# A decoder layer on one core: the eighth pair of the up projection in seven products, with its weight sums formed during the attention and kept in DRAM

## The chip, the core and the metric

The kernel runs on one core of a Trainium2 chip. The core has five engines that run their own instruction streams and meet at semaphores: TensorE (PE: matmuls, with the weight loads in front of them), VectorE (DVE), ScalarE (ACT), GpSimd (POOL) and SyncE (SP), which in this kernel issues nearly all DMAs. Each stream is worked off in the order in which it was built. The metric is the device time of one execution in microseconds (us); lower is better.

## The reference

```python
def reference(x, norm_attn_g, w_in, ..., w_up, w_down):
    h = rmsnorm(x, norm_attn_g)
    proj = einsum('bsd,de->bse', h, w_in)      # q_a k_a v_a | q_b k_b v_b
    o_a = swa_attention(q_a, k_a, v_a, sinks, rel_bias)
    o_b = stick_breaking_attention(q_b, k_b, v_b)
    x = x + concat(rmsnorm(o_a), rmsnorm(o_b)) @ w_out
    h = rmsnorm(x, norm_mlp_g)
    return x + square(relu(h @ w_up)) @ w_down
```

All is float32, with 512 tokens, D = 2048, an MLP width of 8192, and 16 heads of 64 in each of the two groups.

## The kernel before

Each float32 operand of a large product is split into a rounded part `hi` (a copy on ScalarE) and a rest `lo` (a subtraction on VectorE, line 92, or 106 in the first projection). A product is then three matmuls: hi·hi, hi·lo, lo·hi.

**Attention.** `w_in` is read in chunks of two 128-row blocks by 512 columns, `st` (pool `wst`, four buffers), which `wchunk` loads on the SP queue and splits. The stages in order: `kv`, `qa0`, `qa1`, `v0`, two of `qk`, `v1`, two of `qk`; eight chunks each, with 24 matmuls of 512 columns to a chunk. The four results of a stage stand in the four PSUM banks of pool `pp`; the next stage's matmuls write the same banks once VectorE has evacuated them (`f_q`, line 319, for `qa0`). The scores and softmaxes of earlier stages are woven in by `pump`. Before the first softmax the relative-position bias is written to DRAM as a skewed table (`skew`, 3 MB, one DMA on the ACT queue) and read back on the SP queue (`bias`, line 425). The scheduler of the framework, not the program text, settles where each instruction stands in its engine's stream.

**Up projection.** The 16 blocks of 128 rows of `w_up` go in eight pairs (k = 0 to 7), the 8192 columns in 32 groups g of 256. Half of the tokens (256) times two blocks of rows and two of columns is a 2x2 by 2x2 block product. For k = 0 to 6 it is done in seven block products in place of eight (`U_PRODUCTS`), with sums of weight blocks formed by GpSimd (`u_sums`, line 779, four operations) and sums of activation blocks formed once (`turn_x2`, line 754). For k = 7 (`PLAIN`) it is done in eight (`U_PLAIN`). So a group has 7 x 21 + 24 = 171 matmuls of 256 columns. `u_load` fetches two pairs in one DMA (`st_u`, tag `st`, four buffers), `u_sums` forms the sums of two pairs in `s_u` (two buffers; for k = 7 none, so half the width for that tile), `u_split` splits. `u_finish` puts the banks of the group before together, squares the positive part, forms sums for the next product and stores hi and lo to DRAM (`ac`).

**Down projection.** Seven products again, with weight sums by GpSimd (`T1` to `T4`, line 931); the first of them are formed while the last group of the up projection still runs.

Of the kernel before, what the change touches and what calls it, by code (L numbers as in the profile page):

```python
# [12 lines left out]
F32 = mybir.dt.float32  # L13
# [7 lines left out]
P = 128  # L21
# [37 lines left out]
def hymba_layer(ctx: ExitStack, tc: tile.TileContext, x, norm_attn_g, w_in, q_norm_g, k_norm_g,  # L59
# [304 lines left out]
    const.tile([P, 32], F32, name="pad_left")  # L364
# [332 lines left out]

    HP = T // 2
    KP = KD // 2
    PLAIN = KP - 1  # L700
# [15 lines left out]
    def evac_b(n, t, ps):  # L716
# [4 lines left out]
        xs = xw.tile([P, 512], F32, tag="xs", bufs=8, name=f"xs2_{n}{t}")  # L721
# [15 lines left out]
    def turn_x2(n, kk, banks):  # L737
# [3 lines left out]
        for r in range(2):  # L741
# [5 lines left out]
            nc.scalar.mul(out=hq[:, 1:3] if r else hq[:, 0:4:3] if k == PLAIN else hq[:, 0::7],  # L747
                          in_=tr.rearrange("p (b t) -> p b t", b=2), mul=g)
        nb = 4 if k == PLAIN else 7
        hi = hp[k].tile([P, nb, HP], F32R, name=f"h2h{k}")  # L750
        lo = hp[k].tile([P, nb, HP], F32R, name=f"h2l{k}")
        if k != PLAIN:
            for o, a, b in ((3, 7, 0), (4, 2, 3), (5, 2, 7), (6, 1, 4)):
                nc.vector.tensor_tensor(out=hq[:, o], in0=hq[:, a], in1=hq[:, b], op=ALU.subtract)
        split(hq[:, 0:nb], hi, lo)
# [4 lines left out]
    raws, sums, parts_u = {}, {}, {}  # L760
# [8 lines left out]
    def u_sums(i):  # L769
        if i < G * KP // 2:  # L770
            w = raws[i]
            s_ = sp.tile([P, 2, 4, P], F32, tag="s", name=f"s_u{i}")
            if i % (KP // 2) == PLAIN // 2:
                w, s_ = w[:, 0:1], s_[:, 0:1]
            for o, a, b, op in ((s_[:, :, 0], w[:, :, 0], w[:, :, 2], ALU.add),
                                (s_[:, :, 2], w[:, :, 1], w[:, :, 0], ALU.subtract),
                                (s_[:, :, 1], s_[:, :, 0], w[:, :, 1], ALU.subtract),
                                (s_[:, :, 3], w[:, :, 3], s_[:, :, 1], ALU.subtract)):
                nc.gpsimd.tensor_tensor(out=o, in0=a, in1=b, op=op)  # L779
# [16 lines left out]

    U_PLAIN = ((1, 0, 1, 0), (3, 1, 1, 0), (1, 3, 3, 0), (3, 2, 3, 0), (0, 0, 3, 1), (2, 1, 3, 1), (0, 3, 0, 1),
               (2, 2, 0, 1))
    U_PRODUCTS = ((0, 0, 0, 0), (2, 1, 1, 0), (1, 6, 3, 1), (3, 3, 2, 0), (5, 5, 2, 1), (4, 4, 1, 1), (6, 2, 3, 0))

    def u_products(i, ps):
# [3 lines left out]
        for a, b, n, half in U_PLAIN if k == PLAIN else U_PRODUCTS:  # L805
# [9 lines left out]
    def u_finish(g, ps, ew):  # L815
# [3 lines left out]
        p1 = ew.tile([P, HP], F32, tag="p1", name=f"p1_{g}")  # L819
        e = ew.tile([P, 5, HP], F32, tag="e", name=f"e{g}")  # L820
        u = ew.tile([P, 2, HP], F32, tag="u", name=f"u{g}")
        nc.scalar.copy(out=p1, in_=w[:, 0])
        nc.vector.tensor_tensor(out=e[:, 1::3], in0=p1.rearrange("p (o t) -> p o t", o=1).broadcast_to([P, 2, HP]),
                                in1=x_, op=ALU.add)
# [168 lines left out]
    for g in range(1, G):  # L993
        finishing = u_finish(g - 1, ps, ew)
        ps = u_banks(g)
        for k in range(KP):
            if g == G - 1:
# [3 lines left out]
                elif k == 4:  # L1001
                    d_sum(0, "T1")
# [86 lines left out]
```

## Time and profile before

| | |
|---|---|
| median of 3 runs | 2043.79 us (2041.43 to 2044.12) |
| profiled execution, its own time | 2043.11 us |
| its span, first to last instruction | 2041.0 us |
| TensorE busy | 2004.0 us, 98% of the span |
| VectorE, ScalarE, GpSimd busy | 1626.8, 1014.5, 1020.3 us |
| mean granted TensorE clock | 0.996 |

The profiled execution lies 0.7 us under the median. A busy time is the union of an engine's instructions; matmuls overlap, so the time from one matmul's start to the next is what a matmul costs, not its own duration. Times in the rows count from the start of the span.

### The profile page before, as it was taken

The numbers are of one execution on the slowest core, as the hardware profiler recorded it, in microseconds if no ns is written. First come the engines' busy times: TensorE is split into PE (matmuls) and PEld (weight loads), VectorE is DVE, ScalarE is ACT, GpSimd is POOL, SyncE is SP. The second block draws the span as 40 slices with busy tenths as digits, with TensorE's granted clock in tenths as the row PEclk, the third lists the DMA queues.
The fourth block names the chain that finished last, engine by engine and source line by source line (L and its number), as shares of the span: only waits on it lengthen the run. The fifth ranks groups of instructions, "written<-read, shape, count | busy, mean of one in ns | idle before, by whom it ended". The sixth has DMA issues, their size and how long they took to land. (4 is left out here: it accounts for less than half of the span.)

```text
span 2041.0 us, 31132 instructions
## 1 busy us (share of the span) xinstructions
PE 2004.0 (98%) x11748; PEld 1725.3 (85%) x11748; DVE 1626.8 (80%) x2034; ACT 1014.5 (50%) x1676; POOL 1020.3 (50%) x904
## 2 busy tenths in 40 slices
PE   8999999999999999999999999998999999999998
PEld 7887787778677889999999999997788888888887
DVE  4378646665775578999999999998989999999987
ACT  6267534544553565555555555554543333333343
POOL 0014332222320127777777777775756556655654
PEclk9999999999999999999999999999999999999999
DMA  6742332223345555665656565656756557456351
GB/s 220 123 129 85 100 93 81 73 92 111 107 134 186 168 166 182 203 203 183 203 182 205 182 205 182 206 182 264 273 223 227 177 216 267 155 226 258 145 186 62
DMA packets 213914, 350.30 MB, mean 172 GB/s; under 512 B 9779, under 2 KB 154372, under 8 KB 206596
## 3 DMA queue, kind: packets, MB, share of 16 engines
q1 hardware_dynamic: 211216, 345.02, 49.8%
q10 hardware_dynamic: 2548, 3.30, 1.3%
q8 instruction: 92, 1.51, 0.3%
q14 instruction: 58, 0.48, 0.1%
HBM read 270.16 MB, written 78.12 MB: 171 GB/s over the span
## 5 line engine op out<-in xcount | busy, mean ns | idle before, releaser
L811 PE MATMUL ps_u<-h2h,lo_u 128*128 128x256 f32 x1824 | 515.9, 283 | 6.3 <-DVE lo_u L92 6.3
L810 PE MATMUL ps_u<-h2l,hi_u 128*128 128x256 f32 x1824 | 514.7, 282 | 2.4 <-DVE h2l L92 2.4
L809 PE MATMUL ps_u<-h2h,hi_u 128*128 128x256 f32 x1824 | 514.8, 282 | 0.1
L1053 PE MATMUL ps_d<-hi_d,ad 128*128 128x512 f32 x896 | 353.4, 394 | 3.4 <-ACT U L969 1.6
L1054 PE MATMUL ps_d<-lo_d,ad 128*128 128x512 f32 x896 | 353.4, 394 | 1.2 <-DVE lo_d L92 1.2
L1055 PE MATMUL ps_d<-hi_d,ad 128*128 128x512 f32 x896 | 353.2, 394 | 0.0
L811 PEld LDWEIGHTS ps_u<-h2h,lo_u 128*128 128x128 f32 x1824 | 346.7, 190 | 7.5 <-DVE lo_u L92 6.7
L810 PEld LDWEIGHTS ps_u<-h2l,hi_u 128*128 128x128 f32 x1824 | 346.6, 190 | 2.9 <-DVE h2l L92 2.8
L809 PEld LDWEIGHTS ps_u<-h2h,hi_u 128*128 128x128 f32 x1824 | 346.6, 190 | 0.3 <-ACT h2h L91 0.3
L779 POOL TENSOR_TENSOR s_u<-st_u 128x256 f32<-128x256 f32 (+1 forms) x256 | 200.1, 801 | 252.3 <-DVE lo_u L92 181.2
L92 DVE TENSOR_TENSOR lo_d<-T,hi_d 128x1024 fp32r<-128x1024 f32 x128 | 241.4, 1899 | 38.1 <-ACT hi_d L91 37.4
L931 POOL TENSOR_TENSOR T<-st_d,T 128x1024 f32<-128x1024 f32 x64 | 169.1, 2645 | 201.0 <-DVE lo_d L92 198.5
L91 ACT CAST hi_d<-T 128x1024 fp32r<-128x1024 f32 x128 | 134.4, 1051 | 203.0 <-PE ps_d L1055 177.6
L92 DVE TENSOR_TENSOR lo_u<-st_u,hi_u 128x384 fp32r<-128x384 f32 (+1 forms) x256 | 218.2, 853 | 4.4 <-ACT hi_u L91 4.3
L1053 PEld LDWEIGHTS ps_d<-hi_d,ad 128*128 128x128 f32 x896 | 167.9, 187 | 44.6 <-ACT U L969 2.1
L92 DVE TENSOR_TENSOR lo_d<-st_d,hi_d 128x1024 fp32r<-128x1024 f32 x96 | 193.5, 2028 | 13.7 <-ACT hi_d L91 13.2
L1054 PEld LDWEIGHTS ps_d<-lo_d,ad 128*128 128x128 f32 x896 | 168.0, 188 | 42.0 <-DVE lo_d L92 2.0
L1055 PEld LDWEIGHTS ps_d<-hi_d,ad 128*128 128x128 f32 x896 | 168.0, 187 | 40.1
L92 DVE TENSOR_TENSOR lo_u<-s_u,hi_u 128x512 fp32r<-128x512 f32 x224 | 178.1, 795 | 1.0 <-ACT hi_u L91 1.0
L91 ACT CAST hi_u<-s_u 128x512 fp32r<-128x512 f32 x224 | 138.5, 618 | 78.7 <-POOL s_u L779 78.6
L91 ACT CAST hi_d<-st_d 128x1024 fp32r<-128x1024 f32 x96 | 100.6, 1050 | 152.2 <-PE ps_d L1055 140.6
L779 POOL TENSOR_TENSOR s_u<-st_u,s_u 128x256 f32<-128x256 f32 (+1 forms) x128 | 167.8, 1311 | 10.0
(223 smaller groups left out, 3825.7 us busy)
## 6 DMA issues: line engine op xcount, KB each, us to landing
st_u<-in_w_up SPq DMA_DIRECT2D x128, 512.0 KB, 4.5
st_d<-in_w_down SPq DMA_DIRECT2D x64, 1024.0 KB, 8.3
ad<-ac SPq DMA_DIRECT2D x56, 1024.0 KB, 5.1
ac<-ah SPq DMA_DIRECT2D x32, 896.0 KB, 6.3
ac<-al SPq DMA_DIRECT2D x32, 896.0 KB, 6.6
st_qk<-in_w_in SPq DMA_DIRECT2D x64, 256.0 KB, 3.0
st_o<-in_w_out SPq DMA_DIRECT2D x32, 512.0 KB, 4.5
st_qa<-in_w_in SPq DMA_DIRECT2D x16, 512.0 KB, 4.1
```

The lines of the kernel that those rows point to most:

```text
L91: nc.scalar.copy(out=hi, in_=st)
L92: nc.vector.tensor_tensor(out=lo, in0=st, in1=hi.bitcast(F32), op=ALU.subtract)
L779: nc.gpsimd.tensor_tensor(out=o, in0=a, in1=b, op=op)
L809: nc.tensor.matmul(o, wh[:, a], hh[:, b], start=first, stop=False, skip_group_check=True)
L810: nc.tensor.matmul(o, wh[:, a], hl[:, b], start=False, stop=False, skip_group_check=True)
L811: nc.tensor.matmul(o, wl[:, a], hh[:, b], start=False, stop=(k == KP - 1), skip_group_check=True)
L931: nc.gpsimd.tensor_tensor(out=o, in0=raw[cj, a, h], in1=raw[cj, b, h], op=ALU.subtract)
L1053: nc.tensor.matmul(o, al, bh[:, kk], start=first, stop=False, skip_group_check=True)
L1054: nc.tensor.matmul(o, al, bl[:, kk], start=False, stop=False, skip_group_check=True)
L1055: nc.tensor.matmul(o, ar, bh[:, kk], start=False, stop=end, skip_group_check=True)
```

## The change

The eighth pair is done in seven products too. Its weight sums (one tile of 128 x 4 x 128 for each of the 32 column groups) are formed by GpSimd from an extra load of the two row blocks of `w_up`, stored to a DRAM table `us`, and loaded in the up projection into the half of `s_u` that stood empty. The program text calls `sum_ahead` at every second chunk of the eight stages after `kv`, once per column group. `turn_x2` forms the activation sums of the eighth pair as for the others. `u_finish` works in one tile `a` in place of `p1`, `e`, `u` and `a`, with one addition less. `T1` of the first down tile is ordered behind the last weight sums. Some pads and one buffer count (`xs`, 8 to 5) make room.

```diff
+    us = dram.tile([DFF // 256, P, 4, P], F32, name="us")
+    ahead_g = iter(range(DFF // 256))
+    pre = attn.enter_context(tc.tile_pool(name="pre", bufs=2, side="right"))
+
+    def sum_ahead():
+        g = next(ahead_g, None)
+        if g is None:
+            return
+        r = pre.tile([P, 4, P], F32, tag="r", name=f"pr{g}")
+        nc.sync.dma_start(out=r.rearrange("p (k r) c -> p k (r c)", k=2),
+                          in_=w_up.rearrange("(k p) c -> p k c", p=P)[:, KD - 2:KD, g * 256:(g + 1) * 256])
+        z = pre.tile([P, 4, P], F32, tag="z", name=f"ps_{g}")
+        block_sums(r, z)
+        nc.sync.dma_start(out=us[g], in_=z)
+
+    def block_sums(w, z):
+        for o, a, b, op in ((0, w[..., 0, :], w[..., 2, :], ALU.add), (2, w[..., 1, :], w[..., 0, :], ALU.subtract),
+                            (1, z[..., 0, :], w[..., 1, :], ALU.subtract),
+                            (3, w[..., 3, :], z[..., 1, :], ALU.subtract)):
+            ins = nc.gpsimd.tensor_tensor(out=z[..., o, :], in0=a, in1=b, op=op)
+        return ins
...
             hi, lo = wchunk(src(c), f"{name}{c}", perm)
+            if c % 2:
+                sum_ahead()
...
-            if i % (KP // 2) == PLAIN // 2:
-                w, s_ = w[:, 0:1], s_[:, 0:1]
...
+            if i % (KP // 2) == KP // 2 - 1:
+                nc.sync.dma_start(out=s_[:, 1], in_=us[i // (KP // 2)])
+                last_sum[0] = block_sums(w[:, 0], s_[:, 0])
+            else:
+                last_sum[0] = block_sums(w, s_)
...
-            if i % KP == PLAIN:
-                split(w, hi[:, 0:4], lo[:, 0:4])
-                return
...
-        for a, b, n, half in U_PLAIN if k == PLAIN else U_PRODUCTS:
+        for a, b, n, half in U_PRODUCTS:
...
-        nc.vector.tensor_tensor(out=e[:, 3], in0=e[:, 3], in1=w[:, 1], op=ALU.add)
...
-                    d_sum(0, "T1")
+                    with tc.issue_after(last_sum[0].ins):
+                        d_sum(0, "T1")
```

**Where the scheduler puts it.** First the SP queue, from the last chunks of `qa0` on; before, it reads (st_qa0_7 is the last chunk of `qa0`, st_qa1_0 the first of `qa1`):

```order
L111 DMA st_qa0_6_853<-in_w_in 128x2x512
L111 DMA st_qa0_7_885<-in_w_in 128x2x512
L425 DMA bias0_1193<-skew_580 128x256 x2
L425 DMA bias1_1363<-skew_580 128x256 x2
L111 DMA st_qa1_0_957<-in_w_in 128x2x512
```

Now the loads (pr0 to pr31, from `w_up`) and stores (tile names ps_0 to ps_31, to `us`) of all 32 sets begin behind the second chunk of `qa0`, take turns with its other chunks up to set 11, and end ahead of `bias`:

```order
L111 DMA st_qa0_1_669<-in_w_in 128x2x512
L307 DMA pr0_677<-in_w_up 128x2x256
L111 DMA st_qa0_2_737<-in_w_in 128x2x512
L307 DMA pr1_777<-in_w_up 128x2x256
L311 DMA us_582<-ps_0_679 128x512
L307 DMA pr2_849<-in_w_up 128x2x256
L111 DMA st_qa0_3_769<-in_w_in 128x2x512
L311 DMA us_582<-ps_1_779 128x512
```

```order
L307 DMA pr30_4927<-in_w_up 128x2x256
L311 DMA us_582<-ps_29_4849 128x512
L307 DMA pr31_5083<-in_w_up 128x2x256
L311 DMA us_582<-ps_30_4929 128x512
L311 DMA us_582<-ps_31_5085 128x512
L452 DMA bias0_1253<-skew_580 128x256 x2
L452 DMA bias1_1431<-skew_580 128x256 x2
L111 DMA st_qa1_0_993<-in_w_in 128x2x512
```

Nothing is spread over the later stages: 64 DMAs stand between the second chunk of `qa0` and the first of `qa1`. On GpSimd all 128 additions likewise stand ahead of its first work for the attention (hl_k0). The streams of PE, VectorE and ScalarE are the same as before up to the up projection. On VectorE the evacuations of `qa0` (f_q00, f_q01) stand behind the splits of the first three chunks of `qa1`, before and now:

```order
L106 TENSOR_TENSOR lo_qa0_7_916<-st_qa0_7_913,hi_qa0_7_915 128x512 x2
L106 TENSOR_TENSOR lo_qa1_0_996<-st_qa1_0_993,hi_qa1_0_995 128x512 x2
L106 TENSOR_TENSOR lo_qa1_1_1028<-st_qa1_1_1025,hi_qa1_1_1027 128x512 x2
L106 TENSOR_TENSOR lo_qa1_2_1124<-st_qa1_2_1121,hi_qa1_2_1123 128x512 x2
L346 SCALAR_TENSOR_TENSOR f_q00_953<-ps_qa0_0_617,rbc_514 128x512
L346 SCALAR_TENSOR_TENSOR f_q01_962<-ps_qa0_1_618,rbc_514 128x512
```

So these too come behind the 64 DMAs, through the loads of st_qa1_0 to st_qa1_2. The third place is VectorE in the first group of the up projection, between the splits of the seventh and the eighth activation pair (h2l6, h2l7). Before:

```order
L92 TENSOR_TENSOR h2l6_7121<-hq6_7107,h2h6_7120 128x1792
L92 TENSOR_TENSOR lo_u7_7207<-st_u3_6919,hi_u7_7206 128x512
L92 TENSOR_TENSOR lo_u8_7239<-st_u4_7012,hi_u8_7238 128x384
L92 TENSOR_TENSOR lo_u8_7239<-s_u4_7174,hi_u8_7238 128x512
L92 TENSOR_TENSOR h2l7_7169<-hq7_7155,h2h7_7168 128x1024
```

Now:

```order
L92 TENSOR_TENSOR h2l6_7383<-hq6_7369,h2h6_7382 128x1792
L92 TENSOR_TENSOR lo_u7_7473<-st_u3_7180,hi_u7_7472 128x384
L92 TENSOR_TENSOR lo_u7_7473<-s_u3_7336,hi_u7_7472 128x512
L92 TENSOR_TENSOR lo_u8_7507<-st_u4_7273,hi_u8_7506 128x384
L779 TENSOR_TENSOR hq7_7417<-hq7_7417 128x256 x3
L92 TENSOR_TENSOR lo_u8_7507<-s_u4_7440,hi_u8_7506 128x512
L779 TENSOR_TENSOR hq7_7417<-hq7_7417 128x256
L92 TENSOR_TENSOR lo_u9_7534<-st_u4_7273,hi_u9_7533 128x384
L92 TENSOR_TENSOR lo_u9_7534<-s_u4_7440,hi_u9_7533 128x512
L92 TENSOR_TENSOR h2l7_7431<-hq7_7417,h2h7_7430 128x1792
```

Four additions, one more weight split and the split of lo_u9 have come ahead of h2l7, and h2l7 is wider. At the end of the up projection GpSimd's T1_00 and T1_01, which stood ahead of the sums s_u126 and s_u127, now stand behind s_u127.

## Rows read from the trace of the kernel before

**Rows 1.** The page's head: span, and busy time of each engine.

```profile
span 2041.0 us, 31132 instructions
PE 2004.0 (98%) x11748; PEld 1725.3 (85%) x11748; DVE 1626.8 (80%) x2034; ACT 1014.5 (50%) x1676; POOL 1020.3 (50%) x904
```

**Rows 2.** SP queue in order of time, 20 to 116 us: start, length, issue.

```profile
27.04 31.05 SPq L111 DMA_DIRECT2D st_qa<-in_w_in  x7
64.57 0.37 SPq L111 DMA_DIRECT2D st_qa<-in_w_in  x1
95.52 1.76 SPq L425 DMA_DIRECT2D bias<-skew  x4
97.39 15.12 SPq L111 DMA_DIRECT2D st_qa<-in_w_in  x8
```

**Rows 3.** The SP queue's own waits, 60 to 100 us: total, times, longest.

```profile
SPq L425 <- DMA skew<-rv: 30.6, 1, 30.6
```

**Rows 4.** Timeline of ACT, DVE and PE, 84 to 108 us, with idle time ahead.

```profile
86.06 1.14 ACT L105 CAST hi_qa<-st_qa 128x512 fp32r<-128x512 f32 x2 [4.58 <-DMA st_qa<-in_w_in]
101.72 1.14 ACT L105 CAST hi_qa<-st_qa 128x512 fp32r<-128x512 f32 x2 [14.51 <-DMA st_qa<-in_w_in]
...
106.28 1.28 DVE L319 SCALAR_TENSOR_TENSOR f_q<-ps_qa,rbc 128x512 f32<-128x512 f32 x2
...
107.57 0.39 PE L116 MATMUL ps_qa<-hT,hi_qa 128*128 128x512 f32 x1
```

**Rows 5.** GpSimd's timeline, 745 to 749 us: one set of sums on 128x128.

```profile
746.14 0.88 POOL L779 TENSOR_TENSOR s_u<-st_u 128x128 f32<-128x128 f32 x2 [12.44 <-DVE lo_u L92]
746.99 0.46 POOL L779 TENSOR_TENSOR s_u<-s_u,st_u 128x128 f32<-128x128 f32 x1
747.52 0.74 POOL L779 TENSOR_TENSOR s_u<-st_u,s_u 128x128 f32<-128x128 f32 x1
```

**Rows 6.** DMA issues by line: count, size, us from issue to landing.

```profile
st_qk<-in_w_in SPq DMA_DIRECT2D x64, 256.0 KB, 3.0
oscr<-o SPq DMA_DIRECT2D x14, 256.0 KB, 2.0
```

**Rows 7.** Stretches: busy time of each engine, granted clock, DMA share, GB/s.

```profile
core 0: us, PE busy (x) PEld busy (x) DVE busy (x) ACT busy (x) POOL busy (x), PEclk, DMA share, GB/s
64.00:80.00 16.00, 16.00 (x76) 13.30 (x75) 8.09 (x15) 7.89 (x14) 1.16 (x1) 1.00 0.88 102
80.00:86.00 6.00, 6.00 (x28) 4.99 (x27) 2.49 (x3) 1.14 (x2) 2.89 (x2) 1.00 0.99 185
740.00:1390.00 650.00, 646.61 (x5424) 644.78 (x5423) 587.36 (x791) 368.57 (x612) 477.90 (x502) 1.00 0.60 194
1397.70:1404.50 6.80, 5.77 (x27) 5.77 (x28) 5.57 (x6) 4.35 (x4) 2.95 (x2) 0.50 0.25 87
```

**Rows 8.** GpSimd's timeline in the up projection: the same tile in following groups.

```profile
851.22 0.89 POOL L779 TENSOR_TENSOR s_u<-st_u 128x128 f32<-128x128 f32 x2
...
892.12 0.88 POOL L779 TENSOR_TENSOR s_u<-st_u 128x128 f32<-128x128 f32 x2
```

**Rows 9.** Instructions by line and shape: count | busy us, mean ns | idle before.

```profile
L92 DVE TENSOR_TENSOR lo_u<-st_u,hi_u 128x384 fp32r<-128x384 f32 x224 | 180.1, 804 | 4.4 <-ACT hi_u L91 4.3
L92 DVE TENSOR_TENSOR lo_u<-s_u,hi_u 128x512 fp32r<-128x512 f32 x224 | 178.1, 795 | 1.0 <-ACT hi_u L91 1.0
L92 DVE TENSOR_TENSOR lo_u<-st_u,hi_u 128x512 fp32r<-128x512 f32 x32 | 38.1, 1191 | 0.0
L754 DVE TENSOR_TENSOR hq<-hq 128x256 f32<-128x256 f32 x28 | 15.6, 596 | 0.4
```

**Rows 10.** VectorE's timeline, 756 to 769 us: splits of the last two activation pairs.

```profile
757.09 2.19 DVE L92 TENSOR_TENSOR h2l<-hq,h2h 128x1792 fp32r<-128x1792 f32 x1 [1.81 <-ACT h2h L91]
...
762.07 1.22 DVE L92 TENSOR_TENSOR h2l<-hq,h2h 128x1024 fp32r<-128x1024 f32 x1 [0.25 <-ACT h2h L91]
```

**Rows 11.** Waits, 1380 to 1410 us: total, times, longest.

```profile
PE ps_u L811 <- DVE lo_u L92: 6.3, 2, 5.4
```

More of the change, by code (lines that the diff above doesn't have):

```diff
@@ L363, in hymba_layer @@
     oscr = dram.tile([2 * 8, P, T], F32, name="oscr")
-    const.tile([P, 32], F32, name="pad_left")
+    const.tile([P, 24], F32, name="pad_left")
     sm.tile([P, 32], F32, tag="pad", bufs=1, name="pad_small")
@@ L523, in v_group @@
             hi, lo = wchunk(src(c), f"v{o}_{c}")
+            if c % 2:
+                sum_ahead()
             for t in range(NT):
@@ L699, in hymba_layer @@
     KP = KD // 2
-    PLAIN = KP - 1
     G = DFF // 256
@@ L720, in evac_b @@
         nc.sync.dma_start(out=x2scr[n, :, t], in_=xt)
-        xs = xw.tile([P, 512], F32, tag="xs", bufs=8, name=f"xs2_{n}{t}")
+        xs = xw.tile([P, 512], F32, tag="xs", bufs=5, name=f"xs2_{n}{t}")
         nc.scalar.activation(out=xs, in_=xt, func=AF.Square, accum_out=ss2[:, t, n:n + 1])
@@ L746, in turn_x2 @@
             g = gT[:, 16 + 2 * k + r:17 + 2 * k + r]
-            nc.scalar.mul(out=hq[:, 1:3] if r else hq[:, 0:4:3] if k == PLAIN else hq[:, 0::7],
+            nc.scalar.mul(out=hq[:, 1:3] if r else hq[:, 0::7],
                           in_=tr.rearrange("p (b t) -> p b t", b=2), mul=g)
[L749 to L755, printed above, removed]
+        hi = hp[k].tile([P, 7, HP], F32R, name=f"h2h{k}")
+        lo = hp[k].tile([P, 7, HP], F32R, name=f"h2l{k}")
+        for o, a, b in ((3, 7, 0), (4, 2, 3), (5, 2, 7), (6, 1, 4)):
+            nc.vector.tensor_tensor(out=hq[:, o], in0=hq[:, a], in1=hq[:, b], op=ALU.subtract)
+        split(hq[:, 0:7], hi, lo)
         h2[k] = hi, lo
     wu = w_up.rearrange("(k p) c -> p k c", p=P)
-    raws, sums, parts_u = {}, {}, {}
+    raws, sums, parts_u, last_sum = {}, {}, {}, [None]
     def u_load(i):
@@ L772, in u_sums @@
             s_ = sp.tile([P, 2, 4, P], F32, tag="s", name=f"s_u{i}")
-            if i % (KP // 2) == PLAIN // 2:
-                w, s_ = w[:, 0:1], s_[:, 0:1]
[L775 to L779, printed above, removed]
+            if i % (KP // 2) == KP // 2 - 1:
[3 more added lines that the diff above has]
+                last_sum[0] = block_sums(w, s_)
             sums[i] = s_
@@ L793, in u_split @@
             split(s_, hi[:, 3:7], lo[:, 3:7])
-    U_PLAIN = ((1, 0, 1, 0), (3, 1, 1, 0), (1, 3, 3, 0), (3, 2, 3, 0), (0, 0, 3, 1), (2, 1, 3, 1), (0, 3, 0, 1),
-               (2, 2, 0, 1))
     U_PRODUCTS = ((0, 0, 0, 0), (2, 1, 1, 0), (1, 6, 3, 1), (3, 3, 2, 0), (5, 5, 2, 1), (4, 4, 1, 1), (6, 2, 3, 0))
@@ L818, in u_finish @@
         w, x_, y, z = [b.rearrange("p (h t) -> p h t", h=2) for b in ps]
[L819 to L824, printed above, removed]
+        a = ew.tile([P, 8, HP], F32, tag="a", name=f"a{g}")
+        nc.scalar.copy(out=a[:, 7], in_=w[:, 0])
+        nc.vector.tensor_tensor(out=a[:, 1:5:3], in0=a[:, 7:8].broadcast_to([P, 2, HP]), in1=x_, op=ALU.add)
         yield
-        nc.vector.tensor_tensor(out=u, in0=e[:, 4:5].broadcast_to([P, 2, HP]), in1=y, op=ALU.add)
+        nc.vector.tensor_tensor(out=a[:, 5:7], in0=a[:, 4:5].broadcast_to([P, 2, HP]), in1=y, op=ALU.add)
         yield
-        nc.vector.tensor_tensor(out=e[:, 0:4:2], in0=u, in1=z, op=ALU.add)
-        nc.vector.tensor_tensor(out=e[:, 3], in0=u[:, 1], in1=y[:, 0], op=ALU.add)
-        nc.vector.tensor_tensor(out=e[:, 3], in0=e[:, 3], in1=w[:, 1], op=ALU.add)
-        a = ew.tile([P, 8, HP], F32, tag="a", name=f"a{g}")
-        nc.scalar.activation(out=a[:, 0:4], in_=e[:, 0:4], func=AF.Relu)
+        nc.vector.tensor_tensor(out=a[:, 0:4:2], in0=a[:, 5:7], in1=z, op=ALU.add)
+        nc.vector.tensor_tensor(out=a[:, 3], in0=a[:, 6], in1=y[:, 0], op=ALU.add)
+        nc.scalar.activation(out=a[:, 0:4], in_=a[:, 0:4], func=AF.Relu)
         yield
```

## The prediction, made before the changed kernel had run

> **What bounds the kernel now.** I read the head of the profile first [rows 1]: TensorE is busy for 2004.0 of the 2041.0 us of the span, so it sets the pace nearly everywhere, and time can be won only by giving it fewer matmuls, or lost by making it wait. The profiled execution took 2043.11 us, 2.1 more than its span and 0.7 under the median; the sum below starts from 2043.1. Then I looked at the two places that the change touches. In the middle of the up projection (the stretch from 740 to 1390) [rows 7] TensorE is busy for 646.6 of 650 us at granted clock 1.00, and VectorE for 587.4 (90%), GpSimd for 477.9. One tile of sums comes back on GpSimd after 40.90 us [rows 8], which is two column groups, so a group takes 20.45 us. It has 171 matmuls: 119.6 ns each. In the attention, the order of instructions in the section on the change puts 64 new DMAs on the SP queue between the second chunk of `qa0` and `bias`. So I read that queue's stretch and the end of `qa0` closely [rows 2 to 4]: this is where a stall could arise.
>
> **What is removed: 11.5 us.** Each of the 32 groups loses one block product of three matmuls: 32 x 3 x 119.6 ns = 11.5 us. This holds only if TensorE stays the pace. VectorE now works 587.4/650 x 20.45 = 18.5 us a group. For the eighth pair it splits 128x384 and 128x512 (0.80 + 0.80 us) in place of one 128x512 of 1.19 [rows 9], +0.4 us, and saves a small addition that I don't count. 18.9 us against TensorE's new 20.09 is 94%: VectorE stays under it, and I take the whole 11.5. With VectorE as the pace instead it would be between 0 and 11.5.
>
> **What is added in the attention: a stall of TensorE.** First, what is queued behind the new DMAs. SP works its list off in order: the first `bias` DMA waited 30.6 us for `skew` [rows 3], went out at 95.52, and the loads of the chunks of `qa1`, behind it, only from 97.39 [rows 2], though their buffers were free long before. The first of these chunks reached ScalarE at 101.72 (14.51 us idle, waiting for that DMA), VectorE splits three chunks and then evacuates `qa0` at 106.28, 0.64 us for each of the two, and TensorE, which needs the freed bank, goes on at 107.57 [rows 4]. The first evacuation ended at 106.92, so there are 0.6 us to spare. If `bias` goes out at B in place of 95.52, TensorE waits B - 96.1.
>
> Second, the price of a set of sums. GpSimd's four additions on 128x128 took 2.12 us from 746.14 to 748.26 [rows 5]. The load has the 256 KB of a chunk, 3.0 us from issue to landing [rows 6]. There are two buffers, and in SP's list the load of set g+1 stands behind the store of set g-1, so it is not issued before the sums of g-1 are done. Two chains thus take turns, each with store issue 0.47 (four `bias` DMAs in 97.39 - 95.52), landing 3.0 and sums 2.12: 5.6 us for two sets, 2.8 for one. The additions alone (0.88 + 0.46 + 0.74, less a little overlap) make 1.84 to 2.1, the floor; my estimate of a high price is 3.35 (sums of 2.5 while VectorE works too, landing of 3.7 under load).
>
> Third, when they run. The first load follows the first chunks (from 27.04 on), at about 28.6 by my estimate; loads of `w_in` lie in front of it, so that its sums end about 36. Taking turns with the chunks of `qa0`, about nine sets should be through by 66. Now `skew` moves on another queue from about 64 to 95.2. The last chunk of `qa0`, issued at 64.57 [rows 2], reached ScalarE only at 86.06, which had waited for it [rows 4]: 21 us in place of 3. The DMA engines were taken at 0.88 and moved only 102 GB/s until 80, then 185 at 0.99 [rows 7]. A load in this stretch is therefore held. I take two holds: set 9, loaded about 66, is summed about 84 to 86; sets 10 and 11, whose loads follow, land with the backlog behind the end of `skew`, summed at 100 to 103. The other 20 sets take 20 x 2.8 = 56 us. B is about 159, TensorE loses about **63 us**. Bounds: no hold, 66 + 23 sets x 2.8 gives B about 130, a loss of 34; one hold, 86 + 22 x 2.8 = 148, a loss of 52; two holds at 3.35, about 172, a loss of 76.
>
> The Trainium skill (DMA: Bandwidth & Descriptors, Queues, rings and completion order) says that a DMA engine takes turns between the queues that have work for it, packet by packet. By that rule `skew` would slow a load, not hold it; B would lie near one hold, at about 150, and the time near 2090. The row on the last chunk of `qa0` speaks against an even turn.
>
> **Smaller terms.** TensorE's clock: of the stretch that follows its 5.4 us wait at the end of the up projection [rows 11], 6.80 us were granted 0.50, that is 1.2 GHz [rows 7]. After a stall of tens of us I expect such a stretch again, at half speed: **+3 us** (half of 6.8 is 3.4; bounds 0 and 3.4).
>
> First group of the up projection: ahead of the end of the last activation split VectorE gets four additions of 0.60 (2.4 us), a weight split of 0.80 + 0.80 in place of 1.19 (0.4), the split of `lo_u9` (1.6), and h2l itself grows from 1.22 to about 2.1 (0.9) [rows 9, 10]. That is 5.3 us, less some 0.8 that I reckon fits into idle time (1.81 and 0.25 us stand ahead of the two h2l): **+4.5 us**, once, as TensorE has nothing else there. Bounds: 2 if the surroundings give way, 6.
>
> End of the up projection: TensorE waited 6.3 us for `lo_u` [rows 11] and then ran at 0.50 for 6.8 us [rows 7]; `T1`, which stood ahead of the last sums on GpSimd, now stands behind them. Between 0 and 6.3 + 3.4 = 9.7 may come back; I take **-3 us**, since the lo_u chain goes through VectorE and ScalarE too, and `T1` is late next.
>
> At nothing: the loads of the ready sums (256 KB, 2 to 3 us by [rows 6], needed two pairs, 2 x 20.45/8 = 5 us, later; else 32 times the excess); ScalarE's one wider copy a group (ScalarE 368.6 of 650 [rows 7]); one buffer for `a` and five for `xs`; the later start of GpSimd's hl_k, behind the stall anyway. Nor is the stall given back: behind it TensorE has the same matmuls, and it is at 98% now.
>
> Sum: 2043.1 - 11.5 + 63 + 3 + 4.5 - 3 = 2099, and 0.7 for the median: **2100 us**.
>
> **The rivals.** (1) *No hold, but a stall*: the sets run on at 2.8 us beside `skew`. For it: from 80 on the engines moved 185 GB/s. Against: the chunk that took 21 us. 2043.8 - 11.5 + 34 + 3 + 4.5 - 3 = 2071. (2) *One hold, or a slowed queue*: a loss of 52 to 57, so 2089 to 2094. (3) *Dear sets*: 3.35 us each behind two holds, a loss of 76 and up, 2112 to 2120. (4) *Hidden, faster than before*: the loads run far enough ahead that GpSimd's additions alone set the price and `skew` holds none. From 33.7 (28.6 + 3.0 + 2.1), a set at up to (95.5 - 33.7)/32 = 1.93 us is out of the way in time: 2043.8 - 11.5 + 4.5 - 3 = 2034. Below 2.17 us a set (B under 103) the stall is worth less than the gain; above, the kernel is slower. For it: the additions' 1.84 to 2.1. Against: two buffers, and a load that waits for a store in the list.
>
> **How the numbers follow.** A difference under 0.2%, some 4.1 us, can't be told from none. Two holds 0.46, one hold or slowed 0.22, no hold 0.17, dear sets 0.10, hidden 0.05. The forecast is the likeliest case. Its own range is 2094 to 2106 (small terms at their bounds). The range for the whole takes in one hold, no hold and most of the dear sets: 2070 to 2118. Faster comes from the hidden case, 0.04; the same, 0.01, from one just above 2.17 us a set; slower 0.95.
>
> **What would show it.** In the changed kernel's timeline: GpSimd's 128 additions in one block from about 33 on, sets 2.8 us apart except for two gaps between 66 and 103; SP's `bias` at about 159; TensorE idle from about 107.6 to 171 and then at clock 0.50 for some us; in the up projection the same tile of sums after 40.2 us in place of 40.90, TensorE still at 99%; in its first group 4 to 5 us more of idle TensorE ahead of the eighth pair; at its end a wait for `lo_u` shorter than 5.4. The prediction is wrong if `bias` goes out before 128 or after 172, if a set takes less than 2.2 us, or if VectorE's share in the up projection reaches 99% and the group stays near 20.4 us.

## The result, and the profile after

The changed kernel took 2098.35 us (median of 4 runs, 2097.51 to 2099.13) against 2043.39 for the kernel before: a ratio of 1.027 with a 95% interval of 1.0253 to 1.0288. It is 55 us slower. The forecast was 2100.

The head of the page of the changed kernel, as [rows 1]:

```profile
span 2095.8 us, 31391 instructions
PE 1991.2 (95%) x11652; PEld 1725.6 (82%) x11652; DVE 1647.8 (79%) x2038; ACT 1024.1 (49%) x1708; POOL 1067.3 (51%) x1032
```

TensorE has 96 matmuls fewer and is busy 12.8 us less, in a span that is 54.8 us longer. The SP queue in order of time, against [rows 2]:

```profile
64.96 4.99 SPq L307 DMA_DIRECT2D pr<-in_w_up  x1
70.00 4.96 SPq L111 DMA_DIRECT2D st_qa<-in_w_in  x1
75.06 16.97 SPq L311 DMA_DIRECT2D us<-ps  x2
92.12 4.15 SPq L307 DMA_DIRECT2D pr<-in_w_up  x2
...
157.12 2.63 SPq L311 DMA_DIRECT2D us<-ps  x2
159.80 1.88 SPq L452 DMA_DIRECT2D bias<-skew  x4
161.78 15.70 SPq L111 DMA_DIRECT2D st_qa<-in_w_in  x8
```

`bias` goes out at 159.80 in place of 95.52, with the loads of `qa1` behind it. Issuing the load at 64.96 and the chunk at 70.00 took 5 us each, where an issue otherwise takes some 0.4. The packets that the DMA engines worked on say what held them. The table `skew` moves on queue q10, all of SP's loads and stores on q1. From 64 to 80 us, before and after:

```profile
q10 hardware_dynamic: 1067, 1.64, 88.2%
```

```profile
q10 hardware_dynamic: 1066, 1.64, 88.6%
```

These are packets, MB and share; q1 has no line, since none of its packets was moved. Counted from the traces, q1 stood still from 61.0 to 80.0 us before and from 60.9 to 80.0 after. From 82 to 94 the changed kernel's two queues took turns:

```profile
q10 hardware_dynamic: 741, 1.14, 75.8%
q1 hardware_dynamic: 716, 1.10, 24.8%
```

What the SP queue waited for (24 to 162 us; total, times, longest), in place of the one wait for `skew` in [rows 3]:

```profile
SPq L311 <- POOL ps L318: 80.2, 31, 11.5
```

ScalarE and TensorE, against [rows 4]:

```profile
94.17 1.14 ACT L105 CAST hi_qa<-st_qa 128x512 fp32r<-128x512 f32 x2 [14.66 <-DMA st_qa<-in_w_in]
106.83 1.14 ACT L105 CAST hi_qa<-st_qa 128x512 fp32r<-128x512 f32 x2 [11.51 <-DMA st_qa<-in_w_in]
165.92 1.14 ACT L105 CAST hi_qa<-st_qa 128x512 fp32r<-128x512 f32 x2 [57.95 <-DMA st_qa<-in_w_in]
```

```profile
172.09 0.77 PE L116 MATMUL ps_qa<-hT,hi_qa 128*128 128x512 f32 x1 [56.04 <-DVE f_q L346]
```

TensorE does the first matmul of `qa1` at 172.09 in place of 107.57: 64.5 us later. The sets on GpSimd: the last one before `skew`'s hold, the three that were held, and two late ones (the first operations of each set):

```profile
64.50 0.88 POOL L318 TENSOR_TENSOR ps<-pr 128x128 f32<-128x128 f32 x2
...
89.83 0.88 POOL L318 TENSOR_TENSOR ps<-pr 128x128 f32<-128x128 f32 x2 [23.50 <-DMA pr<-in_w_up]
...
99.14 0.88 POOL L318 TENSOR_TENSOR ps<-pr 128x128 f32<-128x128 f32 x2 [7.48 <-DMA pr<-in_w_up]
...
100.93 0.88 POOL L318 TENSOR_TENSOR ps<-pr 128x128 f32<-128x128 f32 x2
...
155.29 0.86 POOL L318 TENSOR_TENSOR ps<-pr 128x128 f32<-128x128 f32 x2 [1.14 <-DMA pr<-in_w_up]
...
157.58 0.86 POOL L318 TENSOR_TENSOR ps<-pr 128x128 f32<-128x128 f32 x2 [0.49 <-DMA pr<-in_w_up]
```

Nine sets were through at 66.3, the tenth followed at 91.7, two more by 102.8, and from there 20 sets to 159.4: 2.83 us each. Stretches, against [rows 7]: from the restart, and (the last) two groups late in the up projection:

```profile
core 0: us, PE busy (x) PEld busy (x) DVE busy (x) ACT busy (x) POOL busy (x), PEclk, DMA share, GB/s
172.09:180.00 7.91, 7.91 (x29) 6.43 (x30) 4.60 (x8) 5.51 (x10) 0.00 (x0) 0.82 0.51 161
1260.45:1301.07 40.62, 40.62 (x338) 40.42 (x337) 37.96 (x51) 23.48 (x40) 29.77 (x33) 1.00 0.65 208
```

VectorE's two last activation splits in the first group, against [rows 10], and TensorE behind them:

```profile
822.04 2.02 DVE L92 TENSOR_TENSOR h2l<-hq,h2h 128x1792 fp32r<-128x1792 f32 x1 [1.81 <-ACT h2h L91]
...
831.50 2.03 DVE L92 TENSOR_TENSOR h2l<-hq,h2h 128x1792 fp32r<-128x1792 f32 x1 [0.74 <-ACT h2h L91]
```

```profile
831.52 1.22 PE L826 MATMUL ps_u<-h2h,hi_u 128*128 128x256 f32 x4 [4.49 <-ACT h2h L91]
```

The second split starts 9.46 us behind the first in place of 4.98. The waits of TensorE at the end of the up projection, against [rows 11]:

```profile
PE ps_u L828 <- DVE lo_u L92: 4.9, 2, 4.4
PE ps_d L1068 <- DVE lo_d L92: 4.2, 1, 4.2
```

**Where the 54.8 us of the span lie.** Starts of the first matmul of a stage, counted from the two traces: at the end of `qa` 66.1 behind, at the start of the up projection 65.5 (740.86 and 806.37). The first group took 29.4 us in place of 25.3, +4.0. From the second group to the start of the down projection -5.3. In the down projection, of which the change touches nothing but the place of `T1` and, through the pads, the place of tiles, -9.5. The first two were forecast nearly to the microsecond; the last two not, though they add up to what was forecast. This is what most of the experiments are about.

The time of a group (first matmul to first matmul of the next) and of 84 matmuls of the down projection, counted in the same way, with runs that follow:

```
                       group: early, then late (from group)   mean of 3 to 31   84 matmuls
before                 20.31   20.46 (23)                        20.35       19.45 / 19.59
after                  20.16   20.31 (18)                        20.23       19.04
before, pad_left 24    20.52   20.52                             20.52       19.04
after,  pad_left 16    19.88   20.32 (8)                         20.26       19.45 / 19.60
```

### The profile page after: what moved, and what is told of

The parts are those of the page before. It is cut to its first block, busy times and chain, and to the rows that moved or that the text cites. A ratio compares the mean times of both kernels' runs of the same rounds, so it can differ in the third digit from the quotient of the medians.

```text
span 2095.8 us, 31391 instructions
## 1 busy us (share of the span) xinstructions
PE 1991.2 (95%) x11652; PEld 1725.6 (82%) x11652; DVE 1647.8 (79%) x2038; ACT 1024.1 (49%) x1708; POOL 1067.3 (51%) x1032
## 5 line engine op out<-in xcount | busy, mean ns | idle before, releaser
L826 PE MATMUL ps_u<-h2h,hi_u 128*128 128x256 f32 x1792 | 508.8, 284 | 4.5 <-ACT h2h L91 4.5
L827 PE MATMUL ps_u<-h2l,hi_u 128*128 128x256 f32 x1792 | 509.0, 284 | 0.6 <-DVE h2l L92 0.6
L318 POOL TENSOR_TENSOR s_u<-st_u 128x256 f32<-128x256 f32 (+1 forms) x256 | 234.4, 935 | 265.2 <-DVE lo_u L92 179.8
L1067 PE MATMUL ps_d<-hi_d,ad 128*128 128x512 f32 x896 | 349.3, 390 | 2.8 <-ACT U L982 1.6
L1069 PE MATMUL ps_d<-hi_d,ad 128*128 128x512 f32 x896 | 349.2, 390 | 0.0
L91 ACT CAST hi_u<-s_u 128x512 fp32r<-128x512 f32 x256 | 158.2, 618 | 184.1 <-POOL s_u L318 184.1
L92 DVE TENSOR_TENSOR lo_u<-s_u,hi_u 128x512 fp32r<-128x512 f32 x256 | 238.2, 931 | 8.0 <-ACT hi_u L91 8.0
L92 DVE TENSOR_TENSOR lo_u<-st_u,hi_u 128x384 fp32r<-128x384 f32 x256 | 193.1, 754 | 3.6 <-ACT hi_u L91 3.5
L91 ACT CAST hi_u<-st_u 128x384 fp32r<-128x384 f32 x256 | 130.2, 509 | 37.6 <-PE ps_u L827 32.5
```

The costliest lines, as they stand in the source:

```text
L91: nc.scalar.copy(out=hi, in_=st)
L92: nc.vector.tensor_tensor(out=lo, in0=st, in1=hi.bitcast(F32), op=ALU.subtract)
L318: ins = nc.gpsimd.tensor_tensor(out=z[..., o, :], in0=a, in1=b, op=op)
L826: nc.tensor.matmul(o, wh[:, a], hh[:, b], start=first, stop=False, skip_group_check=True)
L827: nc.tensor.matmul(o, wh[:, a], hl[:, b], start=False, stop=False, skip_group_check=True)
L1067: nc.tensor.matmul(o, al, bh[:, kk], start=first, stop=False, skip_group_check=True)
```

## The experiments

**1 and 2. The pace of a matmul.** In the kernel before, matmuls of 256 columns came every 118.4 ns in pairs 0 to 5 and every 120.0 ns in pairs 6 and 7; in the changed kernel all came at 120.0. In the down projection before, 24 of 168 came at 226 or 227 ns and the rest at 229 to 236; after, nearly all at 226 or 227. The one thing that goes with this in the program is where tiles lie: the pad of 24 columns in place of 32 shifts the whole left side of SBUF by 32 bytes. Weights lie left; the activations of pairs 0 to 5 lie right, those of 6 and 7 left. The addresses in the built programs fit: pairs 0 to 5 have their two operands 32 bytes apart modulo 64 before and alike after, pairs 6 and 7 alike in both, and in the down projection before 24 of 168 are alike, the rest 32 apart.

```diff
 # kernel before
-    const.tile([P, 32], F32, name="pad_left")
+    const.tile([P, 24], F32, name="pad_left")
```

> The kernel before with one number changed: pad_left 24 columns in place of 32, so that every tile of the left side of SBUF (weights, the activations of pairs 6 and 7) lies 32 bytes lower, at multiples of 64 as the right side already does. Theory (the pace of a matmul hangs on whether its two operands lie at the same offset in 64 bytes): every matmul of 256 columns at 120.0 ns, so a group 171 x 0.120 = 20.52 us in place of 20.31, +6.7 us over 32; every one of 512 columns in the down projection at 226.7, 19.04 us for 84 in place of 19.45 to 19.59, -14 us; about 2036 in all, 2034 to 2039. Rival (the pace comes from the seven products, the extra GpSimd work or the DMA traffic): nothing moves, 2042 to 2046, group 20.31, 84 matmuls 19.5.

```diff
 # changed kernel
-    const.tile([P, 24], F32, name="pad_left")
+    const.tile([P, 16], F32, name="pad_left")
```

> The changed kernel with pad_left 16 in place of 24: the left side is 32 bytes off the right side again, as in the kernel before; all else stays. Theory of the offset: pairs 0 to 5 of the up projection at 118.4 ns, a group 20.16 - 126 x 0.0016 = 19.96 us, -6.5 us; 84 matmuls of the down projection 19.5 in place of 19.04, +14 us; about 2106, 2103 to 2108. Rival (the pace belongs to the change itself): 2098 as it is, group 20.16, 84 matmuls 19.04.

Measured: 2035.25 us, ratio to the kernel before 0.9959 (0.9945 to 0.9972), for the first; 2112.8, ratio 1.0346 (1.0331 to 1.036), for the second. The table above has the groups: 20.52 and 19.04 in the first, as expected. Matmuls of the down projection, in the kernel before and in the same kernel with the pad of 24 (the first and last of seven each):

```profile
1702.84 0.39 PE L1053 MATMUL ps_d<-hi_d,ad 128*128 128x512 f32 x1
...
1704.24 0.39 PE L1053 MATMUL ps_d<-hi_d,ad 128*128 128x512 f32 x1
```

```profile
1702.87 0.39 PE L1054 MATMUL ps_d<-lo_d,ad 128*128 128x512 f32 x1
...
1704.23 0.39 PE L1054 MATMUL ps_d<-lo_d,ad 128*128 128x512 f32 x1
```

1.40 and 1.36 us for six steps: 233 and 227 ns. So the pace hangs on the place of the tiles and not on the seven products; the rival falls. In the second run the down projection lost 12.9 us, as expected; but the groups were faster for six groups only and then went back to 20.32, so the 6.5 us did not come, and the up projection began 2.3 us later. Something else sets a second pace there (experiments 8 to 10).

**3 and 4. The stall.** The same sums with their loads ordered behind the chunk where the program text calls for them, and no sums at all:

```diff
+        with tc.issue_after(chunk[0].ins):      # the load of the w_in chunk
             nc.sync.dma_start(out=r..., in_=w_up...)
```

> The changed kernel, but the load of each set of sums is ordered on the SP queue behind the load of the w_in chunk at which the program text calls for it, so that the 32 sets are spread over the eight stages. Theory (TensorE waited for qa1's first chunk, which stood behind 32 sets on SP): bias goes out at 95 to 98, TensorE's wait of 56 us after qa0 is gone; the stall of 65.5 us goes but for 1 to 3 us; 2033 to 2036. Rival (the sets cost DMA bandwidth, SP time and GpSimd time wherever they are): the wait is cut up, 32 times 0.5 to 1 us stay in the attention, 2049 to 2065.

```diff
     def sum_ahead():
+        return
...
-                nc.sync.dma_start(out=s_[:, 1], in_=us[i // (KP // 2)])
+                nc.sync.dma_start(out=s_[:, 1]..., in_=wu[:, KD - 2:KD, g * 256:(g + 1) * 256])
```

> The changed kernel without the sums in the attention: no load, no addition, no store there; the up projection loads the raw last two row blocks of w_up (the same 256 KB a group) in place of the ready sums, so the sums of the eighth pair are left out of what is computed. It gives the price of forming the sums at all. Theory: bias at 95.5 as in the kernel before, 2098.4 - 65.5 = 2033, 2031 to 2035; against the spread version it shows what the sums cost when nothing waits for them, 0 to 3 us. Rival (the seven products themselves cost elsewhere, or the stall is not from the sums): above 2040.

Measured: 2046.64 us, ratio 1.0016 (1.0007 to 1.0024), and 2031.39, ratio 0.9944 (0.9932 to 0.9957). Without the sums the whole change but them is 11 us faster than the kernel before, and of this the offset of the tiles is the larger part (experiment 1: 8 us). Spread, the stall is gone but the attention ends 12.2 us later than without sums (first matmul of the output projection at 522.9 and 510.7). The profiled execution of the spread kernel took 2041.69 us, 5 less than the median, so most executions lose more than that. TensorE's waits between 100 and 515 us, spread and without sums:

```profile
PE z L579 <- DVE b L601: 3.8, 2, 1.9
PE wtr L613 <- ACT b L604: 2.3, 1, 2.3
PE ps_qa L118 <- DVE f_q L349: 1.5, 1, 1.5
PE ptr L512 <- POOL pr L500: 1.0, 2, 0.7
```

```profile
PE wtr L608 <- ACT b L599: 1.6, 1, 1.6
PE z L574 <- DVE b L596: 1.3, 2, 0.7
PE ptr L507 <- POOL pr L495: 0.7, 1, 0.7
```

The waits listed are 5 us longer in the spread kernel. From 420 to 430, where TensorE idled for 1.9 us, its clock was granted at 0.68 on the mean, which costs some 3 us more; the kernel without sums kept 1.00 in the same stage. The rest is not put down to anything here. Both theories were half right: the wait behind 32 sets made the 65 us, and the sets do cost something wherever these orders put them.

**5. The price of a set.** One buffer:

```diff
-    pre = attn.enter_context(tc.tile_pool(name="pre", bufs=2, side="right"))
+    pre = attn.enter_context(tc.tile_pool(name="pre", bufs=1, side="right"))
```

> The changed kernel with one buffer in place of two for the raw weights and the sums formed ahead: one chain in place of two. Theory (the price of a set is the chain of store issue, load landing and sums; two chains halve it): a set takes 0.47 + 3.0 + 2.1 = 5.6 us, twice the 2.8 seen; some 6 to 8 sets are through when skew ends, 24 to 26 follow, bias goes out at 102 + 24 to 26 x 5.6 = 236 to 248 in place of 159.8; 2175 to 2187. Rival (GpSimd's additions or the DMA engines' bandwidth set the price): a set stays near 2.8, bias at 160 to 175, 2098 to 2115.

Measured: 2144.23 us, ratio 1.0498 (1.0484 to 1.0513). Sets late in the queue:

```profile
149.49 0.87 POOL L318 TENSOR_TENSOR ps<-pr 128x128 f32<-128x128 f32 x2 [3.29 <-DMA pr<-in_w_up]
154.62 0.87 POOL L318 TENSOR_TENSOR ps<-pr 128x128 f32<-128x128 f32 x2 [3.32 <-DMA pr<-in_w_up]
```

5.1 to 5.3 us a set in place of 2.83: GpSimd does 1.8 us and then waits 3.3 for the next load. The chain of load and sums sets the price, and the second buffer nearly halves it. That the time came out below 2175 has two reasons: 5.2 and not 5.6 us a set, and in this order `bias` went out at 199.6, with five sets still behind it.

**6. Early sets, stores behind the next load.** One set a chunk from the fourth chunk of `qa1` on:

```diff
+        if late:
+            h, z = late.pop()
+            with tc.issue_after(ins.ins):       # the load of this set
+                nc.sync.dma_start(out=us[h], in_=z)
...
-            if c % 2:
-                sum_ahead()
+            sum_ahead(name, c)                  # none in qa0 and the first three of qa1
```

> The sums at one set per chunk from the fourth chunk of qa1 on (qa1, v0, and the two qk stages behind it), each load ordered behind its chunk's load on SP, and the store of a set ordered behind the load of the next, so that SP hardly waits for sums. Against the spread version (2046.6, 15 us above the one without sums). Theory (the spread version loses its 12 us in the attention because stores hold SP until the sums are done, and because GpSimd's sums stand ahead of the selections of the stick-breaking weights, whose chain TensorE waits for from about 320 on): most of it comes back, 2034 to 2039. Rival (each set costs the same wherever it is put, through DMA and SBUF traffic): 2044 to 2049.

Measured: 2036.13 us, ratio 0.9969 (0.9958 to 0.9979). As the theory said in time; the output projection starts at 516.0, 5.3 us behind the kernel without sums. 4.9 of these are there at the first `qk` stage already, so I took the place for the cause and moved the sets.

**7. The place of the sets.**

```diff
+        if stage not in ("qk0_", "qk1_", "qk3_"):
+            return
...
+            for _ in range(2 if name == "qk1_" else 1):
+                sum_ahead(name, c)
```

> As the early version, but the sets stand elsewhere: one a chunk in the first qk stage, two a chunk in the second, one a chunk in the fourth. The early version reached the first qk stage 4.9 us later than the one without sums, and lost only 0.4 us more up to the output projection. Theory (a set costs by its place: in qa1 and v0 VectorE, ScalarE and GpSimd are crowded with the windowed attention; in the qk stages they are not): output projection at 511 to 513 us, as without sums (510.7), 2031 to 2034. Rival (each set costs SP, DMA or SBUF time wherever it is): 2035 to 2041.

Measured: 2041.66 us, ratio 0.9991 (0.9982 to 0.9999); output projection at 522.6. This theory fell: the `qk` stages are no free place, and two sets a chunk cost 8 us by the first `z` (328.4 and 320.5). Of these, 6.5 fall between the first matmuls of the two `qk` stages (67.5 us in place of 61.0), while the sets ran two a chunk. TensorE waits 2.1 us there for the softmax's `pr`, which GpSimd forms, and its clock was granted at 0.83 on the mean from 280 to 290. What a set costs in general stays open: it was 0.4 us in all for the 19 sets that stood in `qk0` to `v1` in experiment 6, and some 12 us for 32 in this one.

**8 and 9. The second pace in the up projection.** A third buffer for `s_u`, then the activation tiles 32 bytes off besides:

```diff
-    sp = mlp.enter_context(tc.tile_pool(name="sp", bufs=2, side="right"))
+    sp = mlp.enter_context(tc.tile_pool(name="sp", bufs=3, side="right"))
```

> The last one with three buffers in place of two for s_u in the up projection (four xs and smaller pads make room; offsets in 64 bytes stay). In the changed kernel a group takes 20.16 us at first and 20.31 from the 18th on, with a wait of TensorE for lo_u once a group. Theory (a ring with two buffers sets 20.31: GpSimd's s_u waits for VectorE's lo_u, ScalarE's hi_u for s_u, lo_u for hi_u): with a third buffer all groups stay at 20.16, 2 us less than the early version. Rival (VectorE's own work is the second pace): 20.31 from about the 18th group on as before, no change.

```diff
+    mlp.enter_context(tc.tile_pool(name="off_r", bufs=1, side="right")).tile([P, 8], F32, name="off_r")
...
+    left.enter_context(tc.tile_pool(name="off_l", bufs=1)).tile([P, 8], F32, name="off_l")
```

> The last one, and in the up projection all activation tiles lie 32 bytes off (mod 64) the weight tiles, while both lie alike in the down projection. Theory of the offset: every matmul of 256 columns at 118.4 ns, a group 168 x 0.1184 = 19.9 us, if the third s_u buffer has lifted the second pace: 8 us less than the run before. Rival (VectorE is the second pace): groups at 19.9 only until the slack of the buffers is used up (7 groups, as in the run with pad_left 16), then 20.3; 0 to 2 us less. The down projection stays at 19.04 us for 84 matmuls either way.

Measured: 2041.71 us, ratio 0.9992 (0.9983 to 1.0001), and 2048.22, ratio 1.003 (1.002 to 1.0041). The ring of two is not what sets 20.3: with three buffers most groups still took 20.31 to 20.33, and one among every three or four took 21.0, so that the mean was 20.49. What makes these longer was not found, nor the 3.6 us that the output projection lost against experiment 6. In the second run they began at 19.87, fell back after two, and took 20.55. It also lost 5.9 us ahead of the up projection, which the edit was not meant to touch. To make room it has a pad `pad_small` of 16 columns for 32, and in the built program the operands of the attention's products then lie 64 bytes apart modulo 128, where in the run before they are alike. Matmuls of 512 columns in `kv`, `qa` and `qk` came at 233.3 ns on the mean in place of some 228; over the 1152 of `qa` and `qk` that is some 6 us.

**10. VectorE's waits.** In the changed kernel VectorE's `al`, once a group, comes back every 20.30 us even while TensorE does its groups in 20.16:

```profile
889.54 2.56 DVE L858 TENSOR_TENSOR al<-a,ah 128x1792 fp32r<-128x1792 f32 x1
909.84 2.56 DVE L858 TENSOR_TENSOR al<-a,ah 128x1792 fp32r<-128x1792 f32 x1
930.16 2.56 DVE L858 TENSOR_TENSOR al<-a,ah 128x1792 fp32r<-128x1792 f32 x1
```

TensorE gains 0.15 us a group on it until nothing is ahead any more, after 17 groups. What it gains until then is the same at another offset: in the changed kernel 15 groups at 0.15 us (2.2), in experiment 2 five at 0.43 (2.2); in the kernel before 20 at 0.15 (2.9), in experiment 12 ten at 0.29 (2.9). So the second pace does not hang on TensorE's own. VectorE's waits in three late groups (1281.00 to 1341.67):

```profile
DVE a L849 <- ACT a L847: 3.1, 3, 1.0
DVE lo_u L92 <- ACT hi_u L91: 0.8, 3, 0.3
```

56.67 us of work in these 60.67 and 3.9 of waits. Work and waits of any engine fill its time; what counts is that none of VectorE's waits is for TensorE. Early, from 889.54 to 950.46, it has the same two waits, of the same length, and 56.92 us of work in three periods. The edit meant to take the 1.0 us away (on the version of experiment 7, with the offset):

```diff
-        nc.scalar.activation(out=a[:, 0:4], in_=a[:, 0:4], func=AF.Relu)
-        nc.scalar.square(out=a[:, 0:4], in_=a[:, 0:4])
+        nc.scalar.activation(out=a[:, 0:4:3], in_=a[:, 0:4:3], func=AF.Relu)
+        sq = nc.scalar.square(out=a[:, 0:4:3], in_=a[:, 0:4:3])
+        with tc.issue_after(sq.ins):
+            nc.scalar.activation(out=a[:, 1:3], in_=a[:, 1:3], func=AF.Relu)
+            nc.scalar.square(out=a[:, 1:3], in_=a[:, 1:3])
...
+        with tc.issue_after(last_lo[0].ins):    # three of the sums, and al
```

> The last one, with two more edits in the up projection. ScalarE squares the first and last of the four parts ahead of the other two, and VectorE's sums of them and its al are ordered behind the weight splits, so that VectorE need not wait for ScalarE there (1.0 of the 1.3 us that it waits in a group). And the activation tiles lie 32 bytes off the weights (mod 64). Theory (the second pace of 20.3 us is VectorE's stream with its waits, 18.98 us of work and 1.3 of waits): it falls to about 19.3, so all 32 groups take 19.9 us (168 x 118.4 ns) in place of 20.24 on the mean; 10 us less than the run before, 2021 to 2025. Rival (another ring sets 20.3): groups at 19.9 only for the first 6, then 20.3; no gain over the run before, or a small one.

Measured: 2106.55 us, ratio 1.031 (1.0296 to 1.0324). The expectation failed. VectorE's stream of three groups (1111.36 to 1178.96), stretch and waits:

```profile
1111.36:1178.96 67.60, 62.12 (x506) 60.25 (x505) 58.56 (x76) 35.50 (x67) 48.68 (x49) 1.00 0.58 187
```

```profile
DVE lo_u L92 <- ACT hi_u L91: 8.5, 9, 1.9
DVE a L870 <- ACT a L865: 0.5, 3, 0.2
```

The wait for `a` went from 1.0 to 0.2 us a group, but `ah` now stands ahead of a weight copy on ScalarE and VectorE waits for that: its waits grew from 3.9 to 9.0 us in three groups, and its work to 58.56. A group takes 22.5 us. Lengthening VectorE's stream slowed TensorE by as much; that shortening it would free TensorE was not shown.

**11. The place of T1.** On the version of experiment 7:

```diff
-                    with tc.issue_after(last_sum[0].ins):
-                        d_sum(0, "T1")
+                    d_sum(0, "T1")
```

> The placed version with T1 of the first down tile where the kernel before had it, ahead of the last weight sums on GpSimd, in place of behind them. Step of the prediction: the move gives back 3 us (0 to 9.7), so without it 3 us more. Rival (the move only shifts the wait from lo_u at the end of the up projection to lo_d at the start of the down projection, where the kernels with the move lose 13 to 15.5 us between the last group's start and the third down tile against 13 before): no change, or up to 3 us less.

Measured: 2041.51 us against 2041.66 (ratios 0.999, 0.9981 to 0.9999, and 0.9991, 0.9982 to 0.9999): no difference.

**12. The kernel before with the better offsets.** The pad of experiment 1 and the two of experiment 9.

> The kernel before (eight products for the last pair, no sums ahead) with pad_left 24 as in the first experiment (left and right side alike in 64 bytes, the down projection at 19.04 us for 84 matmuls), and two new pads of 32 bytes that put all activation tiles of the up projection 32 bytes off its weight tiles. Theory (offset, and VectorE's stream as second pace, which was 20.46 us a group in the kernel before): groups at 171 x 118.4 = 20.25 us at first, then 20.46 once the slack is used up, against 20.52 in the first experiment; 2 to 3 us less than that, 2032 to 2034, and the fastest kernel of the study. Rival (no second pace in the kernel before): all groups at 20.25, 8.6 us less, 2026 to 2027.

Measured: 2031.48 us, ratio 0.9941 (0.9927 to 0.9954): the fastest of the kernels that compute all of the reference, 11 us under the kernel before, with no change in the work, and as fast as the changed kernel without its sums (2031.39, experiment 4). Groups took 20.16 us up to the 11th and 20.45 from the 13th on: the second pace of the kernel before, as expected. VectorE's `al` goes at that pace from the start:

```profile
842.22 2.02 DVE L846 TENSOR_TENSOR al<-a,ah 128x1792 fp32r<-128x1792 f32 x1 [0.66 <-ACT ah L844]
862.68 2.03 DVE L846 TENSOR_TENSOR al<-a,ah 128x1792 fp32r<-128x1792 f32 x1 [0.66 <-ACT ah L844]
```

## Why the prediction was right, point by point

- **The stall** was right in place, mechanism and size: `bias` at 159.80 (159 forecast), a loss of 64.5 us (63), nine sets by 66, two holds, 2.83 us a set (2.8). Shown by experiments 3 and 4 (without the queue of sets, or without the sets, the stall is gone) and 5 (one chain in place of two). The second hold ended as forecast, at 100 to 103; the first at 91.7 and not 84 to 86. That `skew` is what held the loads is read from the packets: none on SP's queue from 61 to 80 us, while 1086 of `skew` were moved. From 82 to 94 the two queues took turns, 716 packets and 741, and so the load issued by 70 was summed only at 89.8. The Trainium skill (DMA: Bandwidth & Descriptors, Queues, rings and completion order) has the engines take turns packet by packet between the queues that have work; the second stretch agrees with it, the first does not show it. Why SP's queue moved nothing until 80 stays open, and `skew` itself was not moved to try it. The floor of 1.84 us for the additions stands in no row of the prediction, which give 2.1; the one measured is 1.8 (experiment 5).
- **The clock** cost less: it was granted at 0.82 on the mean of the first 7.9 us, so only a part of them at 1.2 GHz (1.4 us more than at full clock), and the stall had grown from 64.5 to 66.1 by the end of `qa`, 1.5 us in place of 3.
- **The first group**: +4.0 for +4.5. TensorE's wait of 4.49 stands where it was expected.
- **The gain of 11.5 us was mis-sized**: the groups gave 20.35 - 20.23 = 0.12 us each, some 4 us. The step that failed is "VectorE stays under it", from a busy share of 94%. The share leaves out the 1.3 us a group in which VectorE, whose order is fixed, waits for ScalarE; with them it needs 20.3. Its work, 18.97 us a group, was forecast well (18.9). Three matmuls less were worth 0.36 us by their step of 120.0 ns as long as there was slack (20.52 to 20.16, experiment 1 and the changed kernel), and 0.15 (20.46 to 20.31) after. The working also took TensorE's period from a row of GpSimd [rows 8]: 20.45 us is the pace of VectorE, on which GpSimd hangs there; TensorE did its groups in 20.31 at that time.
- **The end of the up projection**: the -3 us for `T1` was 0 (experiment 11). The last group did take 27.6 us in place of 29.8, and the first 84 matmuls of the down projection 25.2 in place of 21.1, with a wait of 4.2 for `lo_d`; but with `T1` back in its old place the last group took 27.6 as well, and the wait was 3.6. So the move makes neither. `T1` is late for another reason that the prediction did not look at: the second half of its weights (`st_d`) now stands on the SP queue behind a store of `ac` that waits 14.6 us for ScalarE's `ah`, and goes out 1.3 us ahead of the down projection in place of 22, with the move and without it.
- **Not foreseen**: the -9.5 us of the down projection. The text called the pads something to make room. Experiments 1 and 2 show that it is the pad: alone it gave -10.4 us in the down projection of the kernel before, and taken back it cost 12.9 in the changed one. The pace of the matmuls is worth some -13, and the late `T1` takes 4 of it back.
- **The range** of 2094 to 2106 is not what its small terms at their bounds give: 2043.8 - 11.5 + 63 = 2095.3, with them 2088 to 2105.

The small terms were forecast at -10.0 us without the clock and measured -10.8 (4.0 - 5.3 - 9.5). Part of the closeness of 2100 to 2098 is therefore luck: with the pad that leaves the offset as it was (experiment 2) the same change took 2112.8. The 65 us are not luck.

## What to carry to other kernels

Before work is moved ahead "into idle time", look in the compiled order at what stands behind it on its DMA queue: a load that may be issued at once, but whose successor needs a buffer back, turns the queue into a chain, and its price is about one set's chain divided by the number of buffers. An engine's busy share understates what its stream needs when its order is fixed: add its waits for engines other than the one that it feeds, and see whether its own period is longer than that engine's. VectorE's 93% was such a case. When an edit changes the size of a tile or a pad, compare the step from matmul to matmul in stages that it does not touch.

## What the runs showed of the hardware that was not expected

The step between matmuls of float32 operands rounded for TensorE depends on where the two operands start. The distances are those of the built programs, the start of the moving tile less that of the weights, modulo 128 bytes; the steps are means, in ns, of matmuls that follow one another without a wait.

```
distance     256 columns             512 columns (down projection)
 0           120.0                   226.7
32           116.8 to 117.8          233.3
96           118.3                   233.3
64           not run                 229.0 (in the attention, experiment 9: 233.3)
```

So a distance makes matmuls of 256 columns a little faster and those of 512 slower. That it is the distance was tried by moving whole sides of SBUF (experiments 1, 2 and 12). The expectations speak of 64 bytes; experiment 9 contradicts that, for there operands 64 bytes apart were slow too, and with two different steps, so the distance modulo 128 does not settle it either. Which of the operands matters, and why the sign turns with the length, stays open.

GpSimd's sums slow VectorE: in the changed kernel one and the same weight split took 0.55 us when it began with GpSimd idle and 1.09 us when it began while GpSimd ran its sums. Counted from 840 to 1060 us, the 33 splits of this size that began with GpSimd idle took 0.54 to 0.56 us; of the 54 that began during a sum, half took 1.09 or more.

```profile
1278.85 0.55 DVE L92 TENSOR_TENSOR lo_u<-st_u,hi_u 128x384 fp32r<-128x384 f32 x1
...
1280.47 1.09 DVE L92 TENSOR_TENSOR lo_u<-st_u,hi_u 128x384 fp32r<-128x384 f32 x1
```

```profile
1279.01 2.13 POOL L318 TENSOR_TENSOR s_u<-st_u 128x256 f32<-128x256 f32 x2 [3.04 <-DVE lo_u L92]
```

The Trainium skill (SBUF — State Buffer, SBUF: two separate sides) says that an operation of VectorE with two SBUF inputs and one of GpSimd that reads SBUF hold a shared port in turn; the rows agree with it.
